# Retention block on Trainium2: turning a head's output with four VectorE instructions and sixteen transfers in place of sixteen VectorE instructions

## The chip, the cores and the metric

One Trainium2 chip, one core of it. The metric is device time in microseconds (us) of one execution. Engines are named as in the profile: PE (TensorE), DVE (VectorE), ACT (ScalarE), POOL (GpSimd) and SP (SyncE, which here only issues transfers). SBUF is the on-chip memory of 128 partitions; a PSUM bank holds one 128x512 result of PE.

## The reference, cut to what matters

One encoder layer over 512 tokens of width 1024, in fp32. The part that the change touches is retention with four heads, whose value width is 512:

```python
h = rmsnorm(x, g_mix[l]);  proj = h @ w_in[l]
ret = ret_f + ret_b                        # per head: decayed scores of q and k, times v
mu = jnp.mean(ret, axis=-1, keepdims=True)
var = jnp.mean(jnp.square(ret - mu), axis=-1, keepdims=True)
ret = (ret - mu) * lax.rsqrt(var + EPS)
ret = jnp.transpose(ret, (0, 2, 1, 3)).reshape(b, s, RET_V) * g_ret[l].astype(jnp.float32)
y_r = (ret.astype(dt) * jax.nn.silu(g_sw)) @ w_r_out[l]
merged = jax.nn.sigmoid(gate_a) * y_a + jax.nn.sigmoid(gate_r) * y_r
x = x + merged @ w_o[l]
```

Before it stands a gated convolution that gives y_a, after it a SwiGLU feed-forward net of width 2816 and a last norm.

## The kernel before, in words

**Products.** An fp32 operand is split into a high part, rounded to a format that PE takes at its higher rate, and a low part, the rest. `split` does this with one ACT instruction for the high part (line 203, or 206 with a gain) and one DVE instruction for the low one (line 204, or 207). A product is three matmuls, high by high, high by low and low by high (`mm3`, lines 342 to 344). Most of the large products use seven block products of two-by-two forms in place of eight (lines 383 and 427).

**Weights.** They come from DRAM through SP's queue into a pool of ten raw tiles of 128x1024 (lines 240 and 286), are sometimes added to each other on DVE (line 301), and are split into a pool of five pairs, `whi` and `wlo`. A table of steps says what is loaded and split ahead of which stage, four to two units ahead. Sums of weight quarters are also made in DRAM by transfers on POOL's queue (`sum_step`, lines 272 and 274); four of these sums are asked for where the last token tile of a head is normalised, so for the last head `t_o` copies and adds stand in POOL's order at that place.

**Stages.** The first half of the program makes q, k, v and the gates, stores them to DRAM through POOL's queue, and computes the convolution. The gate of a head, `sg`, holds all its token tiles on 128 partitions. Then a loop over the heads h does, in the order of the program:

- `load_head(h+1)`: a table, q, k (each as high and low part, `qh`, `ql`), v and the gate, through SP's queue (lines 855 and 860). Each goes into a big tile of 128x2048; there are fourteen big tiles, and each load waits until its tile is free.
- `do_pv(h)`: scores by v, one PSUM bank a token tile. For each bank DVE takes statistics (lines 894 to 896), POOL the power -1/2 (line 897), DVE the product with the gate into the gate's own tile (line 903), after which the bank is free, and ACT the scale (line 905).
- `do_scores(h+1)`: q by k in four banks; DVE applies scale and decay (line 873), then split. `split_v(h+1)` splits v.
- `do_t(h)`: `transpose` turns the head's normalised output (512 tokens by 512 features) into features on partitions, with 16 DVE instructions of 32 partitions each (line 218); each takes a block of 32 tokens and one quarter of the features and writes it to that quarter's partitions. Four splits with the gain follow (lines 206, 207).
- for h = 0 the last quarter of the convolution's output product (`do_mix(3)`), for others `do_wr(h-1)`: the output weight W_r of the head before, in two halves of the columns, 48 matmuls each (`token_major`, line 342 to 344), summed up over heads by ACT (line 935, first head) or DVE (line 937). `do_wr(3)` comes after the loop; its sum is multiplied with a gate (line 939).

So W_r of a head runs one head later than its output. The order on each engine is fixed when the program is built, by a scheduler that takes the order of the program and its own estimates; on the chip each engine runs its list in that order and waits where a semaphore makes it wait. Loads of the next head stand in SP's one list with the weight loads, `sum_step` and the stores in POOL's.

In the code that follows `NB` is 4 and `P` is 128.

## Time and profile before

| what | value |
|---|---|
| runs shown | 1023.23, 1690.56 and 1023.7 us; median 1023.7 |
| span of the profiled execution | 1021.7 us |
| time of the profiled execution itself | not given; the page has its span alone |
| mean granted TensorE clock | 0.999 |
| busy: PE, DVE, ACT, POOL | 1013.2, 902.5, 548.4, 151.7 us |
| 16 transposes of a head (line 218) | 11.44 us, so 45.0 us for four heads |

The span runs from the first to the last instruction of the trace; the time of a run is taken outside it. The page counts an engine as busy while it computes; a PE that is busy 99% of the span has only some 8 us of gaps. The chain of waits starts at the last instruction and follows back to what released each. Times in the trace count from the start of the span. For transfers, the time of an issue on SP or POOL stands apart from the time until the data have landed.

### The profile page before, as it was taken

What the parts mean: (1) busy time and instruction counts of PE and PEld (TensorE: products, weight loads), DVE (VectorE), ACT (ScalarE), POOL (GpSimd) and SP (SyncE); (2) the same over time, 40 slices, a digit from 0 to 9 for tenths busy, and PEclk for the clock granted to TensorE, in tenths of its full rate; (3) what the DMA queues carried; (4) which work ended last, traced back from release to release, by engine and by line L of the source; (5) the groups of instructions that cost most, each with busy time, mean ns of one, the idle gap of its engine ahead of it and who ended that gap; (6) DMA issues with size and microseconds to landing.
All of it is one profiled execution on the core that took longest, in us unless ns stands there. A gap on an engine that the chain in (4) does not pass through costs nothing.

```text
span 1021.7 us, 14821 instructions
## 1 busy us (share of the span) xinstructions
PE 1013.2 (99%) x5586; PEld 883.2 (86%) x5586; DVE 902.5 (88%) x1161; ACT 548.4 (54%) x744; POOL 151.7 (15%) x238
## 2 busy tenths in 40 slices
PE   9999999999999999999999999999999999999997
PEld 7888888888888998888888888889998999899986
DVE  7878998979798888797989997999898999889996
ACT  7547665553655455343543325586654565556554
POOL 0030221222122003202122100020001410110011
PEclk9999999999999999999999999999999999999999
DMA  9525587695767657839597855484316562663523
GB/s 354 188 81 185 173 296 212 214 310 162 249 196 238 250 203 268 333 130 349 124 331 294 272 200 169 157 264 132 107 42 242 172 154 83 198 153 104 165 69 98
DMA packets 53992, 202.34 MB, mean 198 GB/s; under 512 B 7392, under 2 KB 7520, under 8 KB 49312
## 3 DMA queue, kind: packets, MB, share of 16 engines
q1 hardware_dynamic: 37600, 137.39, 39.0%
q0 software_dynamic: 16032, 63.71, 21.3%
q8 instruction: 44, 0.72, 0.3%
q10 hardware_dynamic: 288, 0.29, 0.1%
q14 instruction: 28, 0.23, 0.1%
HBM read 162.82 MB, written 57.41 MB: 216 GB/s over the span
## 4 chain that ended last, share of the span: by engine, by line
PE 98%; DVE 1%; ACT 0%; issue 0%; POOL 0%; POOLq 0%; ACTq 0%
PE bank L427 39%; PE bank L383 27%; PE bank L342 10%; PE bank L343 10%; PE bank L344 10%; PE bank L477 0%; PE bank L1053 0%; PE bank L998 0%; PE bank L662 0%; DVE raw L301 0%; DVE big L1296 0%; ACT whi L203 0%; DVE wlo L204 0%; POOL fin L1286 0%; POOL ac L1035 0%
## 5 line engine op out<-in xcount | busy, mean ns | idle before, releaser
L203 ACT CAST whi<-raw 128x1024 fp32r<-128x1024 f32 (+2 forms) x299 | 302.8, 1028 | 265.0 <-PE bank L427 67.1
L204 DVE TENSOR_TENSOR wlo<-raw,whi 128x1024 fp32r<-128x1024 f32 (+2 forms) x300 | 352.7, 1192 | 68.0 <-ACT whi L203 67.7
L383 PE MATMUL bank<-xform,whi 128*128 128x256 f32 x1424 | 258.2, 284 | 0.3 <-ACT whi L203 0.3
L383 PEld LDWEIGHTS bank<-xform,whi 128*128 128x128 f32 x1424 | 222.3, 192 | 2.0 <-ACT t L434 0.8
L383 PE MATMUL bank<-xform,wlo 128*128 128x256 f32 x712 | 200.7, 283 | 0.0
L427 PE MATMUL bank<-whi,big 128*128 128x512 f32 x596 | 187.0, 389 | 0.0
L427 PE MATMUL bank<-whi,xform 128*128 128x512 f32 x496 | 157.1, 390 | 0.0
L301 DVE TENSOR_TENSOR raw<-raw 128x1024 f32<-128x1024 f32 (+1 forms) x128 | 152.0, 1203 | 4.2 <-DMA raw<-wquad 3.3
L383 PEld LDWEIGHTS bank<-xform,wlo 128*128 128x128 f32 x712 | 136.4, 192 | 0.0
L427 PEld LDWEIGHTS bank<-whi,big 128*128 128x128 f32 x596 | 111.9, 188 | 23.8 <-ACT t L434 0.4
L427 PE MATMUL bank<-wlo,big 128*128 128x512 f32 x298 | 115.7, 389 | 0.0
L427 PEld LDWEIGHTS bank<-whi,xform 128*128 128x128 f32 x496 | 93.0, 188 | 19.7 <-DVE xform L204 0.6
L427 PE MATMUL bank<-wlo,xform 128*128 128x512 f32 x248 | 96.5, 389 | 0.0
L434 ACT COPY t<-bank 128x512 f32<-128x512 f32 x105 | 61.0, 587 | 56.3 <-PE bank L383 30.1
L342 PE MATMUL bank<-big,whi 128*128 128x512 f32 x220 | 85.7, 390 | 0.0
L344 PE MATMUL bank<-big,wlo 128*128 128x512 f32 x220 | 85.6, 389 | 0.0
L343 PE MATMUL bank<-big,whi 128*128 128x512 f32 x220 | 85.6, 389 | 0.0
L427 PEld LDWEIGHTS bank<-wlo,big 128*128 128x128 f32 x298 | 56.0, 188 | 11.4
L427 PEld LDWEIGHTS bank<-wlo,xform 128*128 128x128 f32 x248 | 46.6, 188 | 9.6
L342 PE MATMUL bank<-whi,big 128*128 128x512 f32 x128 | 49.8, 389 | 0.0
L343 PE MATMUL bank<-wlo,big 128*128 128x512 f32 x128 | 49.8, 389 | 0.0
L344 PE MATMUL bank<-whi,big 128*128 128x512 f32 x128 | 49.8, 389 | 0.0
(203 smaller groups left out, 1385.8 us busy)
## 6 DMA issues: line engine op xcount, KB each, us to landing
raw<-wquad SPq DMA_DIRECT2D x140, 512.0 KB, 4.7
raw<-wpack SPq DMA_DIRECT2D x42, 512.0 KB, 6.3
t_f<-wquad POOLq DMA_DIRECT2D x12, 512.0 KB, 8.0
z<-t POOLq DMA_DIRECT2D x24, 256.0 KB, 4.5
t_o<-wquad POOLq DMA_DIRECT2D x12, 512.0 KB, 6.7
zform<-z POOLq DMA_DIRECT2D x6, 1024.0 KB, 7.8
v<-t POOLq DMA_DIRECT2D x16, 256.0 KB, 5.7
sg<-t POOLq DMA_DIRECT2D x16, 256.0 KB, 4.8
```

Of the source, the lines that this page charges most:

```text
L203: first = (round or nc.scalar.copy)(hi, src)
L204: low_of[0] = nc.vector.tensor_tensor(out=lo, in0=src, in1=hi.bitcast(F32), op=ALU.subtract)
L301: nc.vector.tensor_tensor(out=t, in0=t, in1=raws[quad, more, u][:, 0:n], op=ALU.add)
L342: nc.tensor.matmul(ps, lh, rh, start=first, stop=False)
L343: nc.tensor.matmul(ps, lh, rl, start=False, stop=False)
L344: nc.tensor.matmul(ps, ll, rh, start=False, stop=last)
L383: nc.tensor.matmul(o, l[:, c], r[:, k], start=start and s == 0 and k == 0 and i == 0, stop=stop and k == 3 and i == 2, skip_group_check=True)
L427: nc.tensor.matmul(pss[tt], l, r[:, c], start=start and k == 0 and i == 0, stop=stop and k == n - 1 and i == 2, skip_group_check=True)
L434: nc.scalar.copy(t, ps)
```

## The change

**What it does.** `transpose` no longer moves data between groups of 32 partitions on DVE. One DVE instruction a token tile turns the 32x32 blocks in place, on all 128 partitions, into a new big tile `t`; then 16 transfers a head, issued on GpSimd, each move 32 partitions by 512 elements (64 KB) within SBUF to the partitions of their quarter. So that tokens come out in order, the gate `sg` is stored with its tokens in another order (by quarter), the scores are split into permuted columns, and W_r takes its token tiles from the new layout. The splits of the turned head (`split_t`) leave `do_t`: they are traced after the stage that follows, and are put behind the latest high and low cast of the program so far; for the last head they are traced inside the second half of `do_wr(2)`, behind the taking of its weights. The loads of the last stage's first forms (`load_z`) are traced after the turn instead of before it.

```diff
     def transpose(out, src):
 
+        t = bigtile()
+        for j in range(NB):
+            o = t.rearrange("p q (i j r) -> p i q j r", i=4, j=4)[:, :, :, j, :]
+            nc.vector.transpose(o, src[:, j, :].rearrange("p (i q c) -> p i q c", i=4, q=4))
         for b in range(4):
             for q in range(4):
-                i = src[32 * b:32 * b + 32].rearrange("p j (i q c) -> p j i q c", q=4, c=32)
-                o = out[32 * q:32 * q + 32].rearrange("p i (j b c) -> p j i b c", b=4, c=32)
-                nc.vector.transpose(o[:, :, :, b, :], i[:, :, :, q, :])
+                nc.gpsimd.dma_start(out[32 * q:32 * q + 32, b, :], t[32 * b:32 * b + 32, q, :])
...
+    def by_quarter(d):
+        return lambda n: d[32 * n:32 * n + 32].rearrange("r j e -> j r e")
...
-        do_quad(vd[h], sgd[h], AF.Silu)
+        do_quad(by_tile(vd[h]), by_quarter(sgd[h]), AF.Silu)
...
-            split(t, p[0][:, mb, :], p[1][:, mb, :])
+            split(t.rearrange("p (b j r) -> p b j r", b=4, j=4),
+                  *(x[:, mb, :].rearrange("p (j b r) -> p b j r", b=4, j=4) for x in p))
...
     def do_t(h, t):
         tt = bigtile()
         transpose(tt, t)
+        return tt
+
+    def split_t(h, tt):
         yr = (bigtile(F32R), bigtile(F32R))
-        for eb in range(4):
-            split(tt[:, eb, :], yr[0][:, eb, :], yr[1][:, eb, :], gret[:, 4 * h + eb:4 * h + eb + 1])
-        return [yr[0]], [yr[1]]
+        with tc.issue_after(hi_of[0].ins), tc.issue_after(low_of[0].ins):
+            for eb in range(4):
+                split(*(x[:, :, P * eb:P * eb + P] for x in (tt, *yr)), gret[:, 4 * h + eb:4 * h + eb + 1])
+        return yr
...
-        else:
-            load_z((1, 2))
         new = do_t(h, t)
+        if h == HEADS - 1:
+            load_z((1, 2))
         if h == 0:
             do_mix(3)
         else:
             if h == HEADS - 1:
                 sgr = [load(t) for t in grd]
-            do_wr(h - 1, yr)
-        yr = new
+            do_wr(h - 1, yr, (lambda: last.append(split_t(h, new))) if h == HEADS - 1 else None)
+        yr = last[0] if last else split_t(h, new)
```

`hi_of` and `low_of` hold the latest high and low cast of `split`, and `issue_after` keeps an instruction behind another in its engine's order.

**How it moves instructions.** A line of the changed kernel has a number 2 to 10 higher than its twin before: the transpose is line 219, the transfers 222, the splits 204, 205, 207 and 208, statistics 900 to 902, the product with the gate 909, the loads 860, 865, 243 and 289, and the sums of W_r 945 to 949.

The first place is SP's list while head 0's output is turned and head 2 is to be loaded (`qh2`, `ql2`, `v2`, `sg2`; `raw` tiles are weights). Before:

```order
L286 DMA raw_4827<-wquad 128x1024
L860 DMA tab_4263<-tab2_221 128x896
L240 DMA raw_4829<-wpack 128x1024
L855 DMA big_4265<-qh2_227 128x2048
L855 DMA big_4267<-ql2_228 128x2048
L240 DMA raw_4830<-wpack 128x1024
L860 DMA tab_4578<-tab3_222 128x896
L286 DMA raw_5028<-wquad 128x1024
```

With the change:

```order
L289 DMA raw_4832<-wquad 128x1024
L865 DMA tab_4268<-tab2_221 128x896
L243 DMA raw_4834<-wpack 128x1024
L243 DMA raw_4835<-wpack 128x1024
L289 DMA raw_5038<-wquad 128x1024
L243 DMA raw_5040<-wpack 128x1024
L865 DMA tab_4588<-tab3_222 128x896
L243 DMA raw_5041<-wpack 128x1024
L289 DMA raw_5108<-wquad 128x1024
L860 DMA big_4270<-qh2_227 128x2048
L860 DMA big_4272<-ql2_228 128x2048
```

Head 2's q and k, before behind one weight load after their table, now stand behind six and the next head's table. The tile that `qh2` takes is also another: it is the one out of which head 0's 16 transfers read, so this load waits for all of them. That of `ql2` comes free with a matmul near the end of `do_mix(3)`.

The second place is DVE's list while head 1's four banks are normalised. Before (the row with `t` is the last split of a convolution form):

```order
L204 TENSOR_TENSOR t_4258<-big,t_4257 128x256
L896 TENSOR_SCALAR bnmv<-bnmv 128x1
L903 SCALAR_TENSOR_TENSOR big<-bank,bnmv,big 128x512
L894 BN_STATS bnst<-bank 128x6
L895 BN_AGGR bnmv<-bnst 128x2
L896 TENSOR_SCALAR bnmv<-bnmv 128x1
L903 SCALAR_TENSOR_TENSOR big<-bank,bnmv,big 128x512
```

With the change:

```order
L205 TENSOR_TENSOR t_4253<-big,t_4252 128x256
L902 TENSOR_SCALAR bnmv<-bnmv 128x1
L909 SCALAR_TENSOR_TENSOR big<-bank,bnmv,big 128x512
L208 SCALAR_TENSOR_TENSOR big<-big,cols_sb 128x4x128 x4
L900 BN_STATS bnst<-bank 128x6 x2
L901 BN_AGGR bnmv<-bnst 128x2
L900 BN_STATS bnst<-bank 128x6
L902 TENSOR_SCALAR bnmv<-bnmv 128x1
L909 SCALAR_TENSOR_TENSOR big<-bank,bnmv,big 128x512
```

Head 0's four low splits (line 208), before directly behind their transposes, now stand between the first and the second bank of head 1. In PE's list `do_wr(0)` begins directly behind the first matmul of each of the four score banks of head 2, and its four banks are the PSUM banks that head 1's four normalisations (line 909) free.

The third place is the last head, on POOL (sums of weight quarters `t_0_o` and `t_2_o`, the transfers of the turned tile, and the loads of `zform`). Before:

```order
L897 TENSOR_TENSOR bnmv<-bnmv,mhalf 128x1
L274 DMA t_0_o<-t_0_o 16x8192
L274 DMA t_2_o<-t_2_o 16x8192
L272 DMA t_0_o<-wquad 64x2048
L272 DMA t_2_o<-wquad 64x2048
L921 DMA zform<-z_249 128x1024
```

With the change:

```order
L903 TENSOR_TENSOR bnmv<-bnmv,mhalf 128x1 x4
L277 DMA t_0_o<-t_0_o 16x8192
L277 DMA t_2_o<-t_2_o 16x8192
L222 DMA big<-big 32x512
L275 DMA t_0_o<-wquad 64x2048
L275 DMA t_2_o<-wquad 64x2048
L222 DMA big<-big 32x512 x15
L931 DMA zform<-z_245 128x2048
```

One of the 16 transfers stands ahead of the two copies into the weight sums, and 15 behind them.

On DVE, for the same head, before:

```order
L218 STREAM_TRANSPOSE big<-big 32x4x4x32 x16
L937 TENSOR_TENSOR big<-bank,big 128x512 x2
L207 SCALAR_TENSOR_TENSOR big<-big,cols_sb 128x512 x4
L937 TENSOR_TENSOR big<-bank,big 128x512 x2
L204 TENSOR_TENSOR wlo<-raw,whi 128x1024
```

With the change (from the last of the four transposes on):

```order
L219 STREAM_TRANSPOSE big<-big 128x4x4x32
L205 TENSOR_TENSOR wlo<-raw,whi 128x1024
L947 TENSOR_TENSOR big<-bank,big 128x512 x4
L205 TENSOR_TENSOR wlo<-raw,whi 128x1024 x2
L947 TENSOR_TENSOR big<-bank,big 128x512 x4
L205 TENSOR_TENSOR wlo<-raw,whi 128x1024
L304 TENSOR_TENSOR raw<-raw 128x1024 x2
L208 SCALAR_TENSOR_TENSOR big<-big,cols_sb 128x4x128 x4
```

The four low splits, before in the midst of the sums of `do_wr(2)`'s first half, now stand behind the sums of both halves, behind a weight split whose high cast waits for the end of `do_wr(2)`, and behind two additions of weights. On ACT the four high splits stand behind that same cast. `do_wr(3)` on PE needs them at once.

More of the change, by code (lines that the diff above doesn't have):

```diff
@@ L198, in block_kernel @@
     low_of = [None]
+    hi_of = [None]
     def split(src, hi, lo, scale=None, round=None):
@@ L357, in feature_major, with token_major @@
             evict(block0 + m, ps)
-    def token_major(lhs, row0, chunks, evict, before=None):
+    def token_major(lhs, evict, behind=None):
         pss = [bank() for _ in range(NB)]
-        n = 4 * chunks
-        for kk in range(n):
-            if kk % 4 == 0:
-                c = Chunk()
-            if before:
-                before(kk)
+        c = Chunk()
+        if behind:
+            behind()
+        for kk in range(4):
             for nb in range(NB):
-                mm3(pss[nb], act_pair(lhs, row0 + kk, slice(nb * P, (nb + 1) * P)),
-                    c.w(kk % 4, 0, 512), kk == 0, kk == n - 1)
+                mm3(pss[nb], tuple(x[:, nb, kk * P:(kk + 1) * P] for x in lhs), c.w(kk, 0, 512), kk == 0, kk == 3)
         for nb in range(NB):
@@ L749, in ev @@
                     nc.scalar.activation(t, t, f)
-                last = store(dst[:, o + tt, :], t)
+                last = store(dst(o + tt), t)
                 if tt and not o:
@@ L757, in ev21 @@
             nc.scalar.activation(t, ps, func_left or AF.Copy)
-            last = store(left[:, 2 + tt, :], t)
+            last = store(left(2 + tt), t)
             if tt:
@@ L769, in block_kernel @@
     for j in range(2):
-        do_quad(gad[j], grd[j], AF.Sigmoid, AF.Sigmoid)
+        do_quad(by_tile(gad[j]), by_tile(grd[j]), AF.Sigmoid, AF.Sigmoid)
     while held:
@@ L925, in block_kernel, with do_wr @@
     ysum, zf = [], {}
-    def do_wr(h, yr):
+    def do_wr(h, yr, behind=None):
         if h == 0:
@@ L939, in ev @@
                     nc.vector.tensor_tensor(out=t, in0=t, in1=sgr[half][:, nb, :], op=ALU.mult)
-            token_major(yr, 0, 1, ev)
+            token_major(yr, ev, behind if half else None)
     mix_quads()
@@ L946, in block_kernel @@
     do_mix(2)
-    yr = None
+    yr, last = None, []
     for h in range(HEADS):
@@ L957, in block_kernel @@
             vv, sg = split_v(nxt[2]), nxt[3]
-        else:
+        new = do_t(h, t)
+        if h == HEADS - 1:
             load_z((1, 2))
-        new = do_t(h, t)
         if h == 0:
```

5 lines of the change are left out of this document (4 added, 1 removed).

## The prediction

> **What bounds the kernel now.** I read the first line of the page and its busy times, then the chain of waits, the list of who waited for whom, and the windows of the stage that changes.
>
> ```profile
> span 1021.7 us, 14821 instructions
> PE 1013.2 (99%) x5586; PEld 883.2 (86%) x5586; DVE 902.5 (88%) x1161; ACT 548.4 (54%) x744; POOL 151.7 (15%) x238
> PE 98%; DVE 1%; ACT 0%; issue 0%; POOL 0%; POOLq 0%; ACTq 0%
> PE bank L477 <- DVE t L474: 1.4, 1, 1.4
> 440.00:605.00 165.00, 165.00 (x729) 136.62 (x729) 151.67 (x228) 58.81 (x80) 26.02 (x42) 1.00 0.72 242
> 850.00:1021.70 171.70, 165.61 (x1080) 151.84 (x1078) 151.69 (x182) 93.16 (x130) 14.60 (x20) 1.00 0.44 124
> ```
>
> The chain is 98% PE. Its longest wait for DVE, 1.4 us, is the very first, before the stages that change. The window rows give from:to, length, then busy time and instructions of PE, its weight loads, DVE, ACT and POOL, granted clock, DMA share and GB/s. From 440 to 605 us, where heads are turned, PE is busy 165.00 of 165.00 us at full clock: no wait there can be removed. Of the 8.5 us of the span in which PE is idle, 6.1 lie after 850 us, in the net and the end, which the change does not touch. What the change can gain is therefore some 2 us at most; what it can lose is every wait that it gives to PE. This window also gives the pace: 729 matmuls in 165 us, 0.226 us each.
>
> **What is removed.** Of a head's 16 transposes, 12 go.
>
> ```profile
> L218 DVE STREAM_TRANSPOSE big<-big 32x512 f32<-32x512 f32 x64 | 45.0, 703 | 1.7 <-ACT big L905 0.8
> 443.03 11.44 DVE L218 STREAM_TRANSPOSE big<-big 32x512 f32<-32x512 f32 x16
> 454.51 2.57 ACT L206 ACTIVATE big<-big,cols_sb 128x512 fp32r<-128x512 f32 x4 [3.21 <-DVE big L218]
> 455.65 2.74 DVE L207 SCALAR_TENSOR_TENSOR big<-big,cols_sb 128x512 fp32r<-128x512 f32 x4
> ```
>
> A transpose of 128 partitions by 512 is not in the trace. If time goes by the elements of a partition it costs the same 0.703 us; if by blocks, four times as much, 2.81 us, and DVE gains nothing. I take 0.703, since the other 512-element row here, the low split over 128 partitions, takes 2.74 / 4 = 0.69. DVE then loses 48 x 0.703 = 33.7 us of work, all beside a PE that is never idle there: worth nothing to the end.
>
> **What is added: 64 transfers on POOL's queue.** Their issue and their landing are bounded by rows of the same queue (the last figure of a landing row is the median time to landing).
>
> ```profile
> L633 POOL DMA_DIRECT2D sg<-t x16: 542/542/566, 103.3 to 231.9; - x16
> L1208 POOL DMA_DIRECT2D ydr<-first_part x8 | 6.8, 1774 | 0.0
> tab<-t POOLq DMA_DIRECT2D x4, 192.0 KB, 2.8
> sg<-t POOLq DMA_DIRECT2D x16, 256.0 KB, 4.8
> t_o<-wquad POOLq DMA_DIRECT2D x12, 512.0 KB, 6.7
> ```
>
> Issue: 0.54 us from the nearest row, 1.77 from the dearest. I take 0.54 to 0.66, so 16 take 9 to 11 us. Landing: 2.8 to 6.7 us; I take 4.5 for pieces of 64 KB between busy weight loads. For head 0 the transposes end at about 443.0 + 4 x 0.7 = 445.9, the transfers at 446 + 11 + 4.5, some 458 to 461; the splits that wait for them come later, in A.
>
> **A: head 1, 471 to 490 us.** q and k of head 2 were issued at 456.58; now they stand behind six weight loads. The last of these had its twin before at 473.90, and `ql2` follows it.
>
> ```profile
> 471.75 0.69 DVE L819 TENSOR_TENSOR big<-bank,big 128x512 f32<-128x512 f32 x1 [0.64 <-PE bank L344]
> 479.85 0.42 DVE L204 TENSOR_TENSOR t<-big,t 128x256 fp32r<-128x256 f32 x1 [2.05 <-DMA z<-t]
> 480.25 0.74 DVE L903 SCALAR_TENSOR_TENSOR big<-bank,bnmv,big 128x512 f32<-128x512 f32 x1
> 482.00 0.74 DVE L903 SCALAR_TENSOR_TENSOR big<-bank,bnmv,big 128x512 f32<-128x512 f32 x1
> 485.47 0.74 DVE L903 SCALAR_TENSOR_TENSOR big<-bank,bnmv,big 128x512 f32<-128x512 f32 x1
> 456.58 0.33 SPq L855 DMA_DIRECT2D big<-qh  x1
> 473.90 0.33 SPq L286 DMA_DIRECT2D raw<-wquad  x1
> big<-qh SPq DMA_DIRECT2D x1, 1024.0 KB, 6.4
> big<-ql SPq DMA_DIRECT2D x1, 1024.0 KB, 8.5
> ...
> big<-qh SPq DMA_DIRECT2D x1, 1024.0 KB, 8.8
> big<-ql SPq DMA_DIRECT2D x1, 1024.0 KB, 10.8
> ```
>
> The two pairs of landing rows are those of heads 3 and 1. Issued at 474.3, q lands at 480.7 to 483.1 and k at 482.8 to 485.1 and a little more. PE ends the last bank before 471.75, then does 48 matmuls of head 1's own product (10.9 us), and needs q at about 482.7; it needs k 15 matmuls later, at 486.1. So the loads cost 0 to 0.4 us.
>
> The splits cost more. In DVE's new list 4 x 0.68 = 2.7 us stand between the first product with the gate (480.25 to 481.0) and the statistics of banks 2 to 4. After 483.7 the rest of the chain follows, statistics, power on POOL, product: its pieces as before, so banks 2 to 4, which became free at 482.7, 484.5 and 486.2, become free at some 485 to 486.5, 486.1 to 487.7 and 486.9 to 488.5. The W_r matmuls want them 7, 10 and 13 matmuls behind 482.7: at 484.3, 485.0 and 485.6. PE waits 1.3 to 2.9 us by the last of the three; I take **2.0**. If the store for which 479.85 waited lands earlier, the wait shrinks toward nothing.
>
> **B: head 2, 505 to 525 us.** q and k of head 3 were issued at 510.50; in the new list they are behind two more weight loads, which wait for a weight tile freed by the ACT casts here.
>
> ```profile
> 510.50 0.33 SPq L855 DMA_DIRECT2D big<-qh  x1
> 512.16 1.11 ACT L203 CAST whi<-raw 128x1024 fp32r<-128x1024 f32 x1
> 520.71 0.70 DVE L894 BATCH_NORM_STATS2 bnst<-bank 128x6 f32<-128x512 f32 x1 [0.89 <-PE bank L344]
> 530.07 11.44 DVE L218 STREAM_TRANSPOSE big<-big 32x512 f32<-32x512 f32 x16
> ```
>
> That cast ends at 513.3, so I put the issue at 513.3 to 513.7. q lands 6.4 to 8.8 later, 519.7 to 522.1; PE wants it at the end of head 2's product, 520.7. k lands at 522.2 to 524.5, wanted at 522.8. PE waits 0 to 1.7 us; I take **0.5**. Head 2's transposes now end at 530.1 + 2.8 = 532.9, its 16 transfers land by 532.9 + 10.6 + 4.5 = 548, and `do_wr(2)` starts at 558.8 (next fence); the first pair of splits takes 0.65 + 0.75. So 9 us are to spare, and this costs nothing unless a transfer takes more than (558.8 - 532.9 - 4.5 - 1.4) / 16 = 1.25 us. Head 1's transfers have longer still.
>
> **C: the last head, 559 to 587 us.** This is the dear place.
>
> ```profile
> 558.79 0.70 DVE L894 BATCH_NORM_STATS2 bnst<-bank 128x6 f32<-128x512 f32 x1 [0.17 <-PE bank L344]
> 560.64 1.03 POOL L274 DMA_DIRECT2D t_o<-t_o  x2
> 561.47 11.45 DVE L218 STREAM_TRANSPOSE big<-big 32x512 f32<-32x512 f32 x16 [0.85 <-ACT big L905]
> 567.94 0.84 POOL L272 DMA_DIRECT2D t_o<-wquad  x1 [6.27 <-DMA t_o<-t_o]
> 569.16 0.78 POOL L272 DMA_DIRECT2D t_o<-wquad  x1 [0.38 <-DMA t_o<-t_o]
> 580.61 1.05 ACT L203 CAST whi<-raw 128x1024 fp32r<-128x1024 f32 x1 [4.15 <-PE bank L344]
> 585.05 2.48 DVE L301 TENSOR_TENSOR raw<-raw 128x1024 f32<-128x1024 f32 x2
> ...
> zform<-z POOLq DMA_DIRECT2D x6, 1024.0 KB, 7.8
> ```
>
> `do_wr(2)` begins at 558.8 and has 96 matmuls, 21.7 us: it ends at 580.5, as the cast at 580.61 shows, which waited for it. `do_wr(3)` wants the low half of the turned head with its third matmul, at 581.3. In the new lists the low splits stand behind this order of work: the cast (580.6 to 581.7), its low split on DVE (1.2, to 582.9), two additions (2.48, to 585.4), then the first low split (0.75, to 586.1). Before, the splits followed the transposes, which ended at 572.9. PE waits 586.1 - 581.3 = **4.8** us, whatever the transfers do, if they are on time. What follows is paced by PE: each split feeds 12 matmuls, 2.7 us, and takes 0.75.
>
> On time means landed by 584.6. POOL waits for the copies of the sums to land, as before (the rows of 567.94 and 569.16), and issues the last 15 transfers from 569.95 on: at 0.54 to 0.66 us each the last goes at 578.0 to 579.9 and lands, at 4.5, by 582.5 to 584.4. So they are on time with some 0.2 us to spare at the upper end. The loads of forms behind them on POOL go out at 580 to 585 and land some 8 us later; the product that reads them follows the 96 matmuls of `do_wr(3)`, at 586 + 22 = 608: no cost.
>
> **Sum.** 2.0 + 0.5 + 4.8 = 7.3 us on the profiled span of 1021.7 us: 1029.0. The median of the runs shown, 1023.7, lies 2.0 us above that span; the forecast for a run is **1031.0 us**. With each term at its lower end (0, 0, 3.5 if the additions go faster in turn) it is 1027; with the upper ones (2.9, 1.7, and a C of 7) 1035.
>
> **A rule weighed.** The trace has POOL's transfers of the whole program in one row, and one wait for a tile that a store on POOL's queue still read:
>
> ```profile
> q0 software_dynamic: 16032, 63.71, 21.3%
>   DVE t L722: 2.7, 1
> ```
>
> 63.71 MB in 21.3% of 16 engines' span is 63.71 MB / (0.213 x 16 x 1021.7 us) = 18.3 KB a us for one engine. The sixteen stores of `sg` now have an outer size of four on the DRAM side. The Trainium skill, "DMA: Bandwidth & Descriptors", section "Rules for kernel authors", says that an outermost size below 16 confines a transfer to that many engines. By that rule a store of 256 KB would use four engines, 64 KB each: an estimate of 3.6 us instead of 0.9, so 2.7 us more to landing. No run here shows it yet.
>
> **Rivals.**
>
> - *The transfers are dear (ends on the other side).* If one costs not 0.6 but p on POOL's queue, C grows by 15 us for each us above 0.67, and head 2's transfers make PE wait from 1.25 on, 16 us for each us. For the row's 1.77: 15 x 1.1 + 16 x 0.52 = 25 us more, about 1056. It makes the kernel slower by 2% from about 1.4 us on (15 x 0.73 + 16 x 0.15 = 13.4). Against it: 16 of 16 `sg` rows between 542 and 566 ns, with DVE as busy as here. For it: 32 rows apiece of 2 KB between partitions of SBUF is a kind that the trace lacks, and in the built program each waits for the one eight before it to land. The Trainium skill, "SBUF — State Buffer", section "SBUF: two separate sides", tells of such a trap: descriptors of GpSimd's transfers cannot be written while certain VectorE copies run. No run here shows it.
> - *Late landing.* The 15 transfers run into the weight loads of 242 GB/s and land after 6.7 us, so with eight under way 0.84 apiece: the last goes at 569.95 + 12.6 = 582.5, lands at 589.2, split at 590.7: C is 9.4 instead of 4.8, about 1036.
> - *Nothing lost.* The waits at A, B and C are taken up by PE's other work or were misread in the order, and gain and loss are within 2 us: 1022 to 1025. It needs the first splits of the last head by 581.3, for which nothing in the new lists speaks. That the turn does not save DVE any time ends here or at the forecast too, since DVE's time is not what ends last.
> - *Stores of `sg` on four engines.* If each store occupies a staging tile 2.7 us longer and DVE and PE wait once or twice a head for it, as DVE did once for a store in the row above, three heads with one such wait cost some 8 us more: 1039. Against it: that wait of 2.7 us cost PE nothing.
>
> **How the numbers follow.** Forecast (1027 to 1035) 0.65; late landing 0.12; dear transfers 0.08, of which 0.05 with p above 1.4 and the rest up to 1044; nothing lost 0.08; `sg` stores 0.07. The range takes in the late landing, the stores and the upper half of the nothing-lost case and leaves out the dearest transfers: **1024 to 1043**. A measurement of this kernel can tell about 2% from no change, 20.5 us: faster would be below 1003.2, for which PE's 1013.2 busy us leave no room, chance 0.01; slower is above 1044.2, chance 0.06 (the 0.05, and 0.01 for late landing and stores together); the same 0.93.
>
> **What would show it.** Right: four transposes a head of about 0.7 us on DVE and 16 POOL issues of about 0.6; PE with a gap of 1 to 3 us near 485, waiting for line 909; PE with a gap of 4 to 6 us near 581 to 586, waiting for the low split (line 208); DVE's busy time some 34 us lower, and the span 5 to 10 us longer. Wrong: no PE gap near 581; POOL issues above 1 us each; a wait of SP's q load for transfers after 475; gaps of PE in the first 240 us, where `sg` is stored.

## The result, and the profile after

The change runs in 1038.8 us (median of four runs, 1035.62 to 1041.4) against 1023.55 before: 1.0143 times as long, 95% interval 1.0115 to 1.0171. One of the four runs before, 1690.56 us, was a slow one, and the ratio goes by the others. The forecast was 1031.0 with a range of 1024 to 1043. The profiled execution is the fastest of the four, 1035.62 us, with a span of 1033.8: 12.1 us longer than the span before. The page of the change (span, busy times, chain):

```profile
span 1033.8 us, 14860 instructions
PE 1017.3 (98%) x5586; PEld 884.1 (86%) x5586; DVE 868.7 (84%) x1113; ACT 548.9 (53%) x744; POOL 186.3 (18%) x302
PE 79%; issue 7%; DVE 6%; DMA 5%; POOL 2%; ACT 1%; POOLq 0%; DVEq 0%; ACTq 0%
```

VectorE does 33.8 us less, as it was to, and the span is longer. The chain of waits, 98% PE before, now runs through transfers and VectorE. And PE itself is busy 4.1 us longer with as many matmuls as before: a part of the loss is slower matmuls, not waiting.

The windows of the change where the last head is turned (from:to, length, busy time of PE, its weight loads, DVE, ACT, POOL, granted clock, DMA share, GB/s):

```profile
580.00:584.00 4.00, 3.62 (x16) 2.65 (x15) 2.95 (x5) 0.30 (x1) 2.99 (x7) 1.00 0.89 266
584.00:588.00 4.00, 0.00 (x0) 0.00 (x0) 3.50 (x4) 0.75 (x1) 2.16 (x4) 0.95 0.95 266
588.00:592.00 4.00, 2.00 (x5) 1.52 (x6) 2.54 (x5) 2.56 (x4) 1.04 (x2) 0.50 1.03 417
592.00:596.00 4.00, 4.00 (x14) 3.16 (x13) 0.72 (x2) 0.00 (x0) 0.53 (x1) 0.70 1.02 424
```

PE does nothing from 583.6 to 590.0, and some 4 us into that the granted clock falls to 0.50; it stays there until 594.4, so the next ten matmuls stand 0.43 us apart instead of 0.227. The rows of that place, engine by engine (the last bracket is the idle time before the row and what ended it):

```profile
583.24 0.39 PE L347 MATMUL bank<-whi,big 128*128 128x512 f32 x1
590.00 0.79 PE L345 MATMUL bank<-whi,big 128*128 128x512 f32 x1 [6.38 <-ACT big L207]
...
583.70 1.04 ACT L204 CAST whi<-raw 128x1024 fp32r<-128x1024 f32 x1 [4.39 <-PE bank L347]
589.23 2.56 ACT L207 ACTIVATE big<-big,cols_sb 128x512 fp32r<-128x512 f32 x4 [4.48 <-DMA big<-big]
...
586.04 2.48 DVE L304 TENSOR_TENSOR raw<-raw 128x1024 f32<-128x1024 f32 x2
589.98 2.74 DVE L208 SCALAR_TENSOR_TENSOR big<-big,cols_sb 128x512 fp32r<-128x512 f32 x4 [1.46 <-ACT big L207]
...
570.16 3.26 POOL L222 DMA_DIRECT2D big<-big  x6
574.31 0.50 POOL L222 DMA_DIRECT2D big<-big  x1 [0.89 <-DMA t_o<-wquad]
579.04 3.95 POOL L222 DMA_DIRECT2D big<-big  x8 [4.23 <-DMA t_o<-wquad]
```

DVE is through with its two additions at 588.5, so the order of the lists alone would have let the low split go then; but ACT's high split waited until 589.23 for a transfer. On POOL the issues are cheap (0.5 us), but the 9th of the 16 stood 4.23 us, until a sum of 512 KB had landed.

The other loss lies more than 300 us earlier, where the gate is stored. The landing row of these stores, which was 4.8 us before, and PE's waits between 90 and 400 us, of which there were none:

```profile
sg<-t POOLq DMA_DIRECT2D x16, 256.0 KB, 8.0
```

```profile
PE bank L426 <- ACT t L433: 0.8, 1, 0.8
PE bank L426 <- DVE wlo L205: 0.7, 2, 0.5
```

By start to start of PE's matmuls the three places in these two rows cost 2.3 us (0.45, 0.82 and 1.02). At A, near 485 us, it is 0.5. So the 12.1 us are: stores 2.3, A 0.5, last head 6.5 of standing and 2.2 of half clock; that makes 11.5. Of the 0.6 left, 0.3 lie in the first matmuls, at 5 to 7 us, ahead of all that the change moves; the rest is in steps of about 0.1.

The theory that the experiments test: three losses, by the stores of the gate, by the last head's wait, and by the clock behind it; and the wait has two causes that are equally late, the order of the splits and the landing of the transfers. The rivals: one cause alone; a clock that falls for another reason than PE's standing still.

### The profile page after: what moved, and what is told of

Its sections match the earlier page's. It is cut to its first block, busy times and chain, and to the rows that moved or that the text cites. A ratio compares the mean times of both kernels' runs of the same rounds, so it can differ in the third digit from the quotient of the medians.

```text
span 1033.8 us, 14860 instructions
## 1 busy us (share of the span) xinstructions
PE 1017.3 (98%) x5586; PEld 884.1 (86%) x5586; DVE 868.7 (84%) x1113; ACT 548.9 (53%) x744; POOL 186.3 (18%) x302
## 4 chain that ended last, share of the span: by engine, by line
PE 79%; issue 7%; DVE 6%; DMA 5%; POOL 2%; ACT 1%; POOLq 0%; DVEq 0%; ACTq 0%
PE bank L426 29%; PE bank L382 27%; PE bank L345 7%; PE bank L346 7%; PE bank L347 7%; DMA sg<-t 2%; DVE wlo L205 1%; DVE raw L304 1%; DMA t_f<-wquad 1%; DMA t_o<-wquad 1%; DMA big<-big 1%; DMA t_o<-t_o 0%; PE bank L476 0%; POOL tab L632 0%; POOL lw L698 0%
## 6 DMA issues: line engine op xcount, KB each, us to landing
zform<-z POOLq DMA_DIRECT2D x6, 1024.0 KB, 11.5
```

## The experiments

Each edit is given against the change. Times are medians; ratios are to the kernel before on the same chip, with the 95% interval. The intervals reach some 0.1 to 0.2% to either side, since the runs of such a kernel lie 2 to 6 us apart.

### One cause at a time: sums_behind, splits_ahead, order_only

`sum_step` for the last head is called behind its last transfer (`moved[0]`) and no longer in `do_pv`:

```diff
         new = do_t(h, t)
         if h == HEADS - 1:
+            for _ in range(4):
+                sum_step(moved[0], "heads")
             load_z((1, 2))
```

> Only POOL's order for the last head is changed: the four transfers for the weight sums stand behind the 16 transfers of the turned head instead of among them. In the profile of the change PE stood still from 583.5 to 590.0 us, and ACT's first high split waited for a transfer until 589.2. Theory A (two causes equally late: the transfers, and the order of the splits on ACT and DVE): the transfers land some 6 to 8 us earlier, by about 582, but the low split still stands behind the weight cast, its low split and two additions, so PE waits for the low half until about 589.3: a gap of about 5.3 us instead of 6.5, and the time falls by 1 to 2 us, to about 1036 to 1038 at the median of the change's runs. Theory B (the transfers alone are late): the gap is under 1 us and the time falls by 8 to 9 us. Theory C (the order of the splits alone): transfers land earlier and nothing changes, gap 6.5.

Measured: 1037.4 us, ratio 1.0133 (1.0115 to 1.0151). ACT, DVE and PE at the place:

```profile
585.67 1.04 ACT L204 CAST whi<-raw 128x1024 fp32r<-128x1024 f32 x1 [4.39 <-PE bank L349]
586.62 2.56 ACT L207 ACTIVATE big<-big,cols_sb 128x512 fp32r<-128x512 f32 x4
...
588.00 2.48 DVE L306 TENSOR_TENSOR raw<-raw 128x1024 f32<-128x1024 f32 x2
590.41 2.73 DVE L208 SCALAR_TENSOR_TENSOR big<-big,cols_sb 128x512 fp32r<-128x512 f32 x4
...
587.39 0.50 PE L347 MATMUL bank<-whi,big 128*128 128x512 f32 x1 [1.80 <-ACT big L207]
591.20 0.80 PE L349 MATMUL bank<-whi,big 128*128 128x512 f32 x1 [3.08 <-DVE big L208]
```

No row waits for a transfer any more: the high split follows the weight cast without a gap, the low split follows the two additions without a gap. The order alone costs 5.2 us of start to start (2.0 and 3.2), as theory A had it, and half clock follows. In this execution the stores cost more than in the change's (PE waited 2.4 us at 119 us), so its time says little; the rows do.

The mirror image puts the splits ahead in the lists and leaves the sums where they are:

In the second half of `do_wr(2)`, `behind` is now the tracing of the last head's splits without `issue_after`:

```diff
-        c = Chunk()
         if behind:
             behind()
+            with tc.issue_after(hi_of[0].ins), tc.issue_after(low_of[0].ins):
+                c = Chunk()
+        else:
+            c = Chunk()
```

> Only the place of the last head's four splits is changed: they are traced ahead of the weights of the second half of do_wr(2), and those casts are put behind them, so the splits stand ahead of the weight casts and additions on ACT and DVE. The sums stay among the transfers on POOL. Theory A (both late): the transfers still land at about 589, so PE's gap stays at 6 to 6.5 us and the time within 1.5 us of the change's 1038.8. Theory B (the transfers alone): the same as A here. Theory C (the order of the splits alone): the gap goes to about 1 us and the time falls by about 8 us.

Measured: 1034.4 us, ratio 1.0114 (1.0091 to 1.0136), 4.4 us under the change where at most 1.5 were expected. This run tells nothing of the two theories: the edit also put the cast of `do_wr(3)`'s first weights behind the splits, and PE waited 4.3 us for that cast instead. The cleaner form traces the splits behind the weights of that half, again without `issue_after`, and holds back only what the first half of `do_wr(3)` (`after`) prefetches:

```diff
-        c = Chunk()
+        if after:
+            with tc.issue_after(hi_of[0].ins), tc.issue_after(low_of[0].ins):
+                c = Chunk()
+        else:
+            c = Chunk()
         if behind:
             behind()
```

> A cleaner form of splits_ahead, which had put the cast of the first weights of do_wr(3) behind the splits too, so that PE waited 4.3 us for that cast: here only the weights of do_wr(3)'s second half of rows are cast behind the last head's splits, and the first ones as in the change. The sums stay among the 16 transfers on POOL. Theory A (transfers late and order late, about equally): the low split is at best ready when the transfers have landed, at 588 to 591, so PE still stands still for 3 to 6.5 us near 584 to 590 and its clock falls to a half; the time is within 2.5 us of the change's 1038.8. Theory C (the order alone): PE's gap is under 1.5 us, the time 1030 to 1031.

Measured: 1038.0 us, ratio 1.0137 (1.0122 to 1.0152). PE, ACT and POOL:

```profile
591.38 0.79 PE L345 MATMUL bank<-whi,big 128*128 128x512 f32 x1 [7.92 <-ACT big L207]
...
590.61 2.56 ACT L207 ACTIVATE big<-big,cols_sb 128x512 fp32r<-128x512 f32 x4 [22.38 <-DMA big<-big]
...
578.17 0.50 POOL L222 DMA_DIRECT2D big<-big  x1 [3.65 <-DMA t_o<-wquad]
583.79 0.50 POOL L222 DMA_DIRECT2D big<-big  x1 [5.12 <-DMA t_o<-wquad]
```

ACT has nothing else ahead of the splits now and stands 22 us for the transfers; POOL's issues wait 3.65 and 5.12 us for the sums, and PE stands for 7.9 us. So the transfers alone are worth the change's whole wait of 6.5 us, and the order alone 5.2 of it.

### Both: order_and_sums

The edits of sums_behind and order_only in one kernel.

> Both edits for the last head: the sums on POOL behind the 16 transfers, and the splits ahead of the later weight casts and additions. Theory A: the transfers land by about 582 as in sums_behind, the low split runs right behind the sums of do_wr(2) on DVE at about 585, PE waits about 1 us, the clock stays at 1.00, and the time falls by 7 to 8.5 us from 1038.8 to about 1030 to 1032, with the stores of the gate as the rest of the loss. If the time falls no further than with sums_behind (1037.4), theory A is wrong.

Measured: 1030.1 us, ratio 1.0053 (1.0039 to 1.0066), clock 0.998 to 0.999 in every run. In its profile PE waits 0.3 and 0.4 us at the place:

```profile
PE bank L349 <- DVE big L208: 0.4, 1, 0.4
PE bank L347 <- ACT big L207: 0.3, 1, 0.3
```

The loss falls by 8.7 us from the change's 1038.8 where each of its two edits alone (sums_behind, order_only) gained under 1.5, so theory A holds and the two single causes fall. What is left are mainly the stores: PE waits 2.6 us near 261, and 0.7 in two waits before that.

### The clock: pe_kept_busy

`warm` is 28 for the first half of `do_wr(3)`, and 0 elsewhere:

```diff
         if behind:
             behind()
+        for _ in range(warm):
+            nc.tensor.matmul(pss[0], c.w(0, 0, P)[0], c.w(0, 0, 512)[0], start=True, stop=True)
```

> The change with 28 more matmuls on PE at the start of do_wr(3), of weights by weights into the first bank, which is then overwritten; they fill the 6.4 us in which PE waits. Theory A (PE's granted clock falls to a half because PE stood still for over 4 us, and comes back some 4.5 us after it works again; that costs 2.2 us in the profiled run, and its length changes from run to run): the clock stays at 1.00 from 580 to 600 us, the end of the wait stays where it is, the time falls by 2 to 3 us from a median of 1038.8 to about 1036, and the runs lie closer together than the change's 1035.6 to 1041.4. Theory B (the clock fell for another reason, such as the load of the transfers): the clock falls all the same near 587 us and the time does not change.

Measured: 1035.1 us, ratio 1.0115 (1.0092 to 1.0139), 3.7 us under the change, though the two intervals overlap. PE's row and the windows:

```profile
583.35 6.51 PE L369 MATMUL bank<-whi 128*128 128x512 f32 x28
591.38 0.50 PE L345 MATMUL bank<-whi,big 128*128 128x512 f32 x1 [1.52 <-ACT big L207]
```

```profile
584.00:588.00 4.00, 4.00 (x19) 3.30 (x18) 3.50 (x4) 0.65 (x1) 2.15 (x4) 1.00 0.98 320
588.00:592.00 4.00, 2.48 (x11) 1.50 (x9) 1.06 (x2) 1.40 (x3) 1.03 (x2) 1.00 1.02 370
```

The wait ends no sooner (591.4), the transfers weigh as much on memory (320 and 370 GB/s in these windows, 266 and 417 in the change's), and the clock stays at 1.00. So it falls because PE stands still, and the rows show it, whatever the time does. One part of the expectation failed: the runs lie as far apart as the change's (1032.1 to 1038.2), so the half clock at this place is not what makes them vary.

### The stores: sg_load_turns, stores_in_four, stores_alone

```diff
-        do_quad(by_tile(vd[h]), by_quarter(sgd[h]), AF.Silu)
+        do_quad(by_tile(vd[h]), by_tile(sgd[h]), AF.Silu)
...
+        for n in range(NB):
+            nc.sync.dma_start(sg[32 * n:32 * n + 32], sgd[h][:, n, :].rearrange("(j r) e -> r j e", r=32))
```

> The gate is stored by token tile as before the change, and the load of a head makes the quarters, by four loads of 32 partitions in place of one. The rest is the change. Theory A (the stores by quarter cost PE 2.3 us before 260 us, since each takes longer to land and holds its staging tile): the PE waits near 117, 123 and 260 us are gone, landing of the stores falls from 8.0 to about 5 us, and do_mix(3) ends near 472 again instead of 474.3; but then DVE's list near 481 to 488 us, with the splits ahead of the statistics, makes PE wait up to 2 us at the place where it cost 0.5, so the time falls by only 0.5 to 2.3 us. Theory B (those waits come from another move of the order, not from the stores): they stay, and the time does not fall.

Measured: 1041.1 us, ratio 1.0178 (1.0161 to 1.0195): slower than the change, against what was expected. The waits of the stores are gone, landing is back at 4.9 us, and PE ends `do_wr(2)` at 581.6, 2.0 us sooner. But it then stands longer:

```profile
594.08 0.79 PE L345 MATMUL bank<-whi,big 128*128 128x512 f32 x1 [12.47 <-ACT big L207]
...
578.97 2.02 SPq L860 DMA_DIRECT2D big<-gr  x2
```

```profile
big<-big POOLq DMA_DIRECT2D x16, 64.0 KB, 8.8
```

The two loads of 1 MB for the last gate follow PE's progress on SP's queue, and went out at 579.0 instead of 581.0, into the middle of the last eight transfers; the sixteen landed in 8.8 us at the median (the change: 6.3). What was won at the stores was lost at the last head, and more. That the loads are the cause is read from these rows here; gate_loads_behind, below, tests it. The wait at A, which I had put at up to 2 us here, stayed at 0.5.

```diff
-        return lambda n: d[32 * n:32 * n + 32].rearrange("r j e -> j r e")
+        return lambda n, t: [store(d[32 * n:32 * n + 32, j, :], t[32 * j:32 * j + 32]) for j in range(4)][-1]
```

> The change, with each store of the gate by quarter split into four stores of 32 rows of 64 KB, so that the outer size of each pattern is 32 and not 4; 64 stores in place of 16. Theory A (a pattern with an outer size of 4 is spread over 4 of the 16 engines, which makes it land late): each piece lands in 3 to 5 us like the transfers of 64 KB, the waits of PE near 117, 123 and 260 us go or shrink below 0.5 us in sum, at the price of 48 more issues of 0.5 us on POOL, which is idle there for 28 us before such stores. do_mix(3) ends near 472. The time moves little, since the last head's wait starts earlier by as much. Theory B (the quarters scatter the writes in DRAM and that is slow): landing stays near 8 us and the waits stay.

Measured: 1033.6 us, ratio 1.009 (1.0076 to 1.0103). The stores' landing and the window in which they lie:

```profile
sg<-t POOLq DMA_DIRECT2D x64, 64.0 KB, 3.7
```

```profile
100.00:265.00 165.00, 165.00 (x729) 136.60 (x729) 144.89 (x160) 91.75 (x116) 60.42 (x113) 1.00 0.73 228
```

The same bytes go to the same places in DRAM, with an outer size of 32 in place of 4, and land in 3.7 us; PE is busy 165.00 of 165.00 us again (the change: 163.51). So scattered writes are not the cause. The edit changed the size of a store too, from 256 to 64 KB, so the outer size is not shown alone; but the pages hold a sign of what the outer size of 4 does:

```profile
DMA packets 59113, 206.57 MB, mean 200 GB/s; under 512 B 11488, under 2 KB 11616, under 8 KB 54432
```

This is the change; before it was 7392 packets under 512 B, and in stores_in_four it is 9184. With 16 for each added transfer (64 of the turn, 48 more stores) the last two agree to the packet. The change has 3072 more than that: 192 for each of its 16 stores, of 8 bytes each in the trace, and they are there in no kernel without such stores. The last head's wait is as it was, 6.4 us.

Finally the stores by quarter alone, in the kernel before, with loads that turn them back:

> The kernel before, with one thing of the change: the gate stored by quarter (16 stores whose DRAM pattern has an outer size of 4), and turned back by the head's loads (four of 32 partitions instead of one). Transposes and splits are as before. Theory A (such a store lands some 3 us later and holds its staging tile): landing 8 us instead of 4.8, waits of PE of 1.5 to 5 us before 262 us, DVE and not PE taking the first of them, and the time 1025 to 1029. Theory B (the stores cost only in the company of the change's other parts): 1023.5.

Measured: 1028.0 us, ratio 1.0046 (1.0031 to 1.0061); landing 7.5 us, PE's longest wait 3.4 us, at 261, with half clock behind it in the profiled execution. This one part of the change, with the loads that turn it back, costs 4.8 us by itself, by the medians.

### All together, and what holds the transfers: all_three, sums_order_stores, last_head_on_sp, gate_loads_behind

The first is order_and_sums with the edit of sg_load_turns.

> order_and_sums, and the gate stored by token tile, with the quarters made by the head's loads, as in sg_load_turns. Theory A (three losses: stores of the gate 2.3 us and more, the last head 6.5 us, and the half clock behind it 2.2 us): with all of them gone the waits near 117 and 260 us are absent, PE waits 1 to 2 us near 582 and under 1 us near 485, and the time is 1024.5 to 1027, within 0.3% of before and not under it, since the VectorE time that is saved lies beside PE. If saved VectorE time were worth something, the time would be below 1023.

Measured: 1029.5 us, ratio 1.005 (1.0038 to 1.0063); no waits at the stores, but 2.6 us at the last head, whose transfers again landed in 6.9 us. Not the expected 1024.5 to 1027.

The second is order_and_sums with the edit of stores_in_four.

> order_and_sums with stores_in_four: the sums behind the last head's transfers, its splits ahead of the later weight casts, and each store of the gate by quarter in four pieces of 32 rows. Theory A: no wait of PE for the stores, as in stores_in_four (do_wr(2) ends near 580), and the last head's wait is what is left of the transfers' landing: they are issued on POOL from 565 to 578 with eight under way and the two 1 MB loads of the gate at 567, and land by 582, so PE waits 1 to 3 us there, without a half clock. Time 1024 to 1027.

Measured: 1025.6 us, ratio 1.0027 (1.0016 to 1.0038); PE waits 1.5 us at the last head and its transfers land in 5.5 us. Two runs then ask why transfers of 64 KB land so late. The first takes stores_in_four and order_only, leaves the sums where they were, and issues the last head's transfers on SP's queue:

```diff
-        transpose(tt, t)
+        transpose(tt, t, nc.sync if h == HEADS - 1 else None)
```

> The change with stores_in_four and the splits ahead of the later weight casts, and with the last head's 16 transfers issued on SP's queue, ahead of the two 1 MB loads of the gate, while the sums stay on POOL where they were. Theory A (the last head's transfers are late because of what stands around them, POOL's waits for the sums and 2 MB of loads beside them, not because of what they are): SP issues one in 0.3 to 0.45 us as it does other loads, from about 566 to 573, they land by 577, PE waits under 1.3 us (for the sums on DVE ahead of the low split), the clock stays at 1.00, and the time is 1022.5 to 1025, not above before by more than 0.2% and not under it by more than 0.1%. Theory B (64 KB between partitions lands late in any case): the wait stays at 2 us or more, 1025 to 1028.

Measured: 1035.7 us, ratio 1.0123 (1.011 to 1.0137). Theory A as I had put it, with a free queue as the cure, is wrong. SP, ACT, and the landing row of the stretch:

```profile
562.33 14.29 SPq L224 DMA_DIRECT2D big<-big  x16
...
586.23 2.56 ACT L207 ACTIVATE big<-big,cols_sb 128x512 fp32r<-128x512 f32 x4 [21.47 <-DMA big<-big]
```

```profile
zform<-z POOLq DMA_DIRECT2D x4, 1024.0 KB, 15.1
t_o<-t_o POOLq DMA_DIRECT2D x2, 512.0 KB, 4.6
big<-big SPq DMA_DIRECT2D x16, 64.0 KB, 8.2
t_o<-wquad POOLq DMA_DIRECT2D x2, 512.0 KB, 9.0
```

POOL, freed of the 16 transfers, sent its sums (2 MB) and four loads of 1 MB by 569, and beside them the transfers landed in 8.2 us each and were done only at 586. The last run is sums_order_stores again, with the transfers on POOL, and keeps the 2 MB of gate loads back until they have landed:

```diff
-                sgr = [load(t) for t in grd]
...
+    with tc.issue_after(hi_of[0].ins), tc.issue_after(low_of[0].ins):
+        sgr = [load(t) for t in grd]
     load_z((3,))
```

> sums_order_stores with the two 1 MB loads of the last gate behind the last head's 16 transfers: they are traced after do_wr(2), and the first of them takes the tile that the transfers read, so it waits for all of them. Theory A (what makes 64 KB land late at the last head is the megabytes that are under way beside it): without these 2 MB the 16 transfers, issued from 562 to 571, land by 575 to 577 instead of 580.4, their median landing falls from 5.5 to 3 to 4 us, PE's wait near 580 falls from 1.65 us to under 1.2 (then the sums of do_wr(2) on DVE ahead of the low split set it), and the time is 1024 to 1025.3 instead of 1025.6. Theory B (a landing of 5 us and more with eight under way is what such transfers take on this queue at that rate): landing and wait stay as they were, 1025.6 again. In no case should it fall under 1022.8, since PE has nothing more to gain there.

Measured: 1025.7 us, ratio 1.002 (1.0011 to 1.0029). The landing row, ACT, DVE and PE:

```profile
big<-big POOLq DMA_DIRECT2D x16, 64.0 KB, 2.8
```

```profile
574.10 2.56 ACT L207 ACTIVATE big<-big,cols_sb 128x512 fp32r<-128x512 f32 x4 [8.37 <-DMA big<-big]
...
578.97 2.73 DVE L958 TENSOR_TENSOR big<-bank,big 128x512 f32<-128x512 f32 x4 [8.15 <-PE bank L349]
581.61 2.73 DVE L208 SCALAR_TENSOR_TENSOR big<-big,cols_sb 128x512 fp32r<-128x512 f32 x4
...
582.41 0.50 PE L349 MATMUL bank<-whi,big 128*128 128x512 f32 x1 [0.99 <-DVE big L208]
```

The same transfers on the same queue land in 2.8 us, and ACT can start at 574.1 instead of 580.5 (sums_order_stores): theory A in its right form, megabytes under way beside them, holds. The time hardly moved (ratio 1.0020 after 1.0027, and the intervals overlap): PE now waits 1.0 us for DVE, whose low split stands behind the sums of `do_wr(2)`. This is the best form found: the change without most of its losses, still 0.2% slower than before, with 34 us less VectorE work. Its span is 3.1 us over that of before: by start to start 0.5 at A, 1.3 at the last head, and 1.1 near 790 us, far behind the turn, where PE waits 1.4 us for a weight cast (0.3 before). That wait is 0.3 in the change's profile and 2.0 in that of last_head_on_sp, so no run shows that it belongs to the change.

## Why the prediction was right and wrong, point by point

**What bounds the kernel** was right: with VectorE's work 34 us shorter and most of the losses taken out, the best form does not beat the kernel before.

**The prices** of the new operations were right. The groups and issues of the change:

```profile
L219 DVE STREAM_TRANSPOSE big<-big 128x512 f32<-128x512 f32 x16 | 10.2, 684 | 0.8 <-ACT big L911 0.8
```

```profile
L222 POOL DMA_DIRECT2D big<-big x64: 496/498/793, 448.7 to 582.5; - x64
```

The transpose over 128 partitions takes 0.684 us, so it goes by the elements of a partition (0.703 was taken); a transfer is issued in 0.50 us (0.54 to 0.66) and lands in 4.8 us at the median of all 64 (4.5), from 1.8 to 9.1. The rival of dear transfers, on which most of the chance of slower by 2% hung, fell. The Trainium skill, "SBUF — State Buffer", section "SBUF: two separate sides", tells that VectorE copies can keep GpSimd from writing descriptors. Here no issue took more than 0.793 us beside a busy VectorE, so the trace shows nothing of it.

**A** was forecast at 2.0 us and cost 0.5. The order did what was said: DVE's rows of the change near there are

```profile
480.69 0.74 DVE L909 SCALAR_TENSOR_TENSOR big<-bank,bnmv,big 128x512 f32<-128x512 f32 x1
481.35 2.73 DVE L208 SCALAR_TENSOR_TENSOR big<-big,cols_sb 128x512 fp32r<-128x512 f32 x4
...
487.57 0.75 DVE L909 SCALAR_TENSOR_TENSOR big<-bank,bnmv,big 128x512 f32<-128x512 f32 x1
```

and the banks became free at 486.6, 487.6 and 488.3, within the forecast's 485 to 488.5. But the 2.05 us that DVE had waited for the `z` store at 479.85 before were no longer there, so its first product came only 0.4 us later than before, while PE came 2.6 us later, most of which it had lost at the stores. That PE was late is not what helped: without the stores' loss, in stores_in_four, PE and the whole row of DVE work lay 3.7 us earlier (that product at 476.97), and PE's loss was again 0.5. The prediction had named the case of that store landing earlier and not taken it. q and k came in time (forecast 0 to 0.4); in the profile of pe_kept_busy k was 0.4 us late.

**B**, 0.5 forecast, cost nothing in the profiled execution.

**C** is the term that was mis-sized: 4.8 us forecast, 8.7 in the profiled execution. The order of the lists costs what was said (5.2 us in sums_behind). Three things were missed. First, "issues the last 15 transfers from 569.95 on: at 0.54 to 0.66 us each" left out that an issue stands behind the landing of the eighth one before it, and that the two sums of 512 KB are among those eight: POOL stood 0.89 and 4.23 us for them. The six transfers issued at 570.2 to 572.7 landed only at 579.3 to 580.5, just behind the second sum (578.8). Second, the last transfers went out together with 2 MB of gate loads, so that ACT got them at 589.2 and not by 584.4. This is the rival of late landing (0.12), whose 9.4 us the term came near. It had the last transfer issued at 582.5 and landed at 589.2, as it was (582.5 and 589.1); but it reckoned with 0.84 us an issue, and the trace has two stands and 0.5 us an issue, so the agreement is luck in part. Third, nothing was said of PE's clock, which falls after such a wait. It costs 2.2 us here. The Trainium skill, "TensorE: Matmul & The Clock Gate", section "What's actually happening", has the rule that I should have put beside C: PE goes to half clock after an idle window of about 3.4 us that runs free of the program, and needs about as much work to come back. The trace agrees: half clock from some 4 us into the wait of 6.4 us until 4.4 us after its end. But the clock fell in a wait of 2.4 us too (sums_behind, last section), which is shorter than the window that the Trainium skill gives, and there the measurement decides.

**The stores of the gate** were held a rival (0.07) and are part of the case: 2.3 us of the profiled execution, and 4.8 us of the median in stores_alone. The rule of the Trainium skill that was weighed there ("DMA: Bandwidth & Descriptors", section "Rules for kernel authors") gave an estimate of 2.7 us more to landing. It is 3.2 (4.8 to 8.0), and with an outer size of 32 it is gone. What failed is the step from landing to PE: I gave the wait to the staging tiles, and argued that such a wait had cost PE nothing. Here DVE waited 6.3 us in four waits for those tiles (in stores_alone 5.9, and ACT 5.4), and PE for DVE and ACT.

**The sum** of 7.3 us was 12.1 in the profiled execution and 15.2 by the medians. A and B came out 2.0 lower, C 3.9 higher, and the 2.3 of the stores were not in it. Nor do the terms always add: a gain at the stores was lost at the last head (sg_load_turns). The range held since it reached to the rivals, so it is luck in part; the chance of the forecast's own case was set too high, and none of the cases had two of the rivals at once, which is what happened. Of the prediction's own signs, the gap near 485 was 0.5 and not 1 to 3, PE at the last head waited for the high split (line 207) and not for the low one, and a sign of being wrong was there: gaps of PE at 117 and 123 us, where `sg` is stored.

What stays open: why executions of one kernel lie 2 to 6 us apart. The stores' waits differ in the profiles of kernels that have the same stores (PE waits from 1.4 to 5.1 us in sum before 265 us), and the runs of the two kernels with neither such stores nor half clock lie within 2.7 and 3.3 us. Two profiles, of splits_ahead and stores_alone, are of the slowest execution of their kernel. Both have the longest of these waits, 3.4 us near 261, with half clock after it; in stores_alone that place costs 5.9 us, and its runs lie 6.1 apart. That points at the stores and the clock, but no faster execution of these two kernels was profiled. That a store by quarter uses four of the sixteen engines was not seen engine by engine; 192 packets are 12 x 16, which would fit twelve engines without data, but the trace does not name engines.

## What to carry to other kernels

Work taken off an engine that lies beside the bounding one was worth nothing here, and each wait that pays for it counts in full: look for where the new steps land in each in-order list, and what stands ahead of them. A transfer's price is not its size but what is under way beside it and in the same queue, so small transfers that something waits for go ahead of large ones, not among them. Where two things are late by the same amount, taking away one shows little; take away both before dropping either.

## What the runs showed of the hardware

PE's granted clock fell to a half during waits of 6.4 to 12.5 us and came back 3.7 to 6.2 us after work began, so that such a wait costs about 2 to 3 us more than it lasts. The clock records of these traces show eleven spells of half clock before the end of the program, and each is 3.4, 6.8, 10.2 or 13.7 us long, one to four times 3.41. The fall came 1.9 to 5.1 us after PE had stopped, and twice 1.2 us after it had begun again (splits_ahead near 264, last_head_on_sp near 800). Shorter waits went both ways: after 2.4 us at 119 us (sums_behind) and after 3.4 us at 261 us (stores_alone) it had fallen, after 2.6 us at 261 us (order_and_sums) and at 583 us (all_three) it had not:

```profile
116.00:120.00 4.00, 1.60 (x6) 1.04 (x5) 4.00 (x7) 2.78 (x5) 2.00 (x3) 0.87 0.18 42
120.00:124.00 4.00, 4.00 (x14) 3.14 (x13) 4.00 (x4) 1.82 (x2) 1.07 (x2) 0.70 0.72 152
```

These are the windows of sums_behind; the granted clock, the third figure from the end, is 0.87 and then 0.70.

Transfers of 64 KB between partitions of SBUF landed in 2.8 us with little beside them, in 5.5 with 2 MB of loads and in 8.2 with some 6 MB, the first two on POOL's queue and the last on SP's. A store of 256 KB landed in 4.8 us with an outer size of 128 in its pattern and in 8.0 with one of 4; in four pieces of 32 rows it landed in 3.7. Only the stores with an outer size of 4 brought 192 extra packets of 8 bytes each.
